# Triangular inverses in a linear-attention encoder: elimination on blocks of 16 and two joins on TensorE, in place of elimination on blocks of 32 and one join

## Chip, cores and metric

One Trainium2 chip, one of its cores. The metric is the device time of the whole program in microseconds (us); lower is better. All arithmetic is in 32-bit floats; the large products split each operand into a high and a low part and use three matmuls.

## The reference

An encoder layer runs on two sequences of 512 and 256 tokens, held together as T = 768 columns: a mixer (half RWKV-7, half gated linear attention, GLA), cross attention, and a feed-forward network. The change lies in the RWKV-7 part. Each of its 8 heads carries a 64x64 state through time, forward and backward:

```python
def step(S, inp):
    r_t, w_t, k_t, v_t, kk_t, a_t = inp
    sa = jnp.einsum('bhij,bhj->bhi', S, -kk_t)
    S = (S * w_t[:, :, None, :] + sa[..., None] * (kk_t * a_t)[:, :, None, :]
         + v_t[..., None] * k_t[:, :, None, :])
    return S, jnp.einsum('bhij,bhj->bhi', S, r_t)
```

The kernel does this in chunks of 64 tokens. Within a chunk the corrections `sa` of all tokens depend on one another through a strictly triangular 64x64 matrix L, so the kernel needs the inverse of (I - L) for every chunk, head and direction: 12 chunks x 2 heads x 2 directions for each of 4 pairs of heads.

## The kernel before

Work is written in program order and then ordered by a planner, which has a cost model of each instruction and a priority that the code sets with `tc.high_priority(offset=...)`. Each engine then runs its own list in order. All transfers go through one queue, that of SP.

The mixer handles four pairs p of heads:

- `begin(p)` prepares a pair: decays, the scaled keys `bk`, and `lower`, which makes L on TensorE (L685), copies it to the tile `lsb`, and writes its diagonal blocks to the DRAM tensor `ld`.
- `invert(p)` calls `inverses`. It loads the diagonal 32x32 blocks so that one partition holds one block (48 forward blocks on partitions 0 to 47, 48 backward ones, flipped, on 64 to 111). It builds the inverse in `sqf` by elimination on VectorE: 31 steps, each a multiply into `stmp` (L744) and an add (L746). The inverse goes to the DRAM tensor `qd`, its transpose to `td`.
- `joined(p)` calls `join`. It loads both back in the layout of the matrices (`tt` holds the 64x64 result, `tdz` a transposed block), multiplies the off-diagonal 32x32 block of L with the inverses on its two sides (L788, copied by ScalarE at L792; then L800, copied by VectorE at L803), and writes the 64x64 inverse to `ttd`.
- `products(st, g)` loads the pieces of a group of chunks from DRAM, `ttd` among them, into the tiles `pl`, and makes the matrices of the recurrence. `stage(q)` runs the recurrence over chunks in four steps (L1018 to L1064), pair q and part of pair q - 1 together.

Around them lie dense projections (`gla_dense`, `rkv_early`, L247), the four GLA heads, and 16 `memory_block`s (L1104), which the planner may put between other work. The program order of the pairs is: begin, invert and join 0; pair 1 among the GLA heads; begin and invert 2; stage 0; begin 3, join 2, invert 3; the memory blocks; stage 1; join 3; stages 2, 3 and 4. An inverse is therefore always written after the join of the pair before, with which it shares `sqf`.

The tiles `snf`, `sqf` and `sxf`, each 1,024 floats a partition, later hold weights of the output projection and its gain row `g_post`.

Of the kernel before, what the change touches and what calls it, by code (L numbers as in the profile page):

```python
# [8 lines left out]
F32 = mybir.dt.float32  # L9
F32R = mybir.dt.float32r  # L10
# [6 lines left out]
P = 128  # L17
D = 1024
# [14 lines left out]
def kernel(ctx: ExitStack, tc: tile.TileContext, I, y_prompt, y_sample):  # L33
# [354 lines left out]
    for v in ("w0_f", "w0_b", "a0_f", "a0_b", "k_k", "k_a", "lnx_w", "lnx_b"):  # L388
# [214 lines left out]

    mp_cm = tc.tile_pool(name="mp", bufs=1, reuse_waits="tile")
    mp = mp_cm.__enter__()
    tts, tdz = [], []
    for d in range(2):
        t = mp.tile([P, NCH, 64], F32, tag=f"tt{d}", name=f"tt{d}")
        pool.memset(t, 0.0)
        tts.append(t)  # L610
        tdz.append(mp.tile([P, NCH, 32], F32, name=f"tdz{d}"))
# [5 lines left out]
    sn, sq, sx = snf[0:112], sqf[0:112], sxf[0:112]  # L617
    stmp = mp.tile([112, 256], F32, name="stmp")
    pool.memset(sn, 0.0)

    def pt_(tag, bufs=1):
# [56 lines left out]
    def lower(st, d, b_, a_):  # L678

        lt = mp.tile([P, NCH, 64], F32, tag="lsb", bufs=4, name="lsb")  # L680
        for c0, n in ((0, 8), (8, 4)):
            pm = psn("low").rearrange("p (c x) -> p c x", x=64)
            for c in range(n):
                for h, hs in enumerate(HS):
                    pe.matmul(out=pm[hs, c, :], lhsT=b_[hs, c0 + c, h, :], rhs=a_[hs, c0 + c, h, :],  # L685
                              start=True, stop=True)
# [44 lines left out]
    def inverses(st):  # L731


        flat = fl
        ld, qd, td = (x[st["p"]] for x in (lds, qds, tds))
        dma(sn[0:48], ld[0].rearrange("s b c t -> (b c) s t"))
        dma(sx[64:112], ld[1].rearrange("s b c t -> (b c) s t"))
        dve.tensor_copy(out=flat(sn[64:112]), in_=flat(sx[64:112])[:, ::-1])
        dve.memset(sq, 0.0)
        dve.memset(flat(sq)[:, 0:1024:33], 1.0)  # L740
        for j in range(31):
            nr, ni = j + 1, 31 - j
            tm = stmp[:, 0:nr * ni].rearrange("p (a b) -> p a b", a=nr)
            dve.tensor_tensor(out=tm, in0=sq[:, 0:nr, j:j + 1].broadcast_to([112, nr, ni]),  # L744
                              in1=sn[:, j:j + 1, j + 1:32].broadcast_to([112, nr, ni]), op=ALU.mult)
            dve.tensor_tensor(out=sq[:, 0:nr, j + 1:32], in0=sq[:, 0:nr, j + 1:32], in1=tm, op=ALU.add)  # L746
        dma(qd[0].rearrange("s b c t -> (b c) s t"), sq[0:48])
        dve.tensor_copy(out=sn[0:48], in_=sq[0:48].rearrange("p a b -> p b a"))
        dma(td[0].rearrange("s b c t -> (b c) s t"), sn[0:48])
        dve.tensor_copy(out=flat(sx[64:112]), in_=flat(sq[64:112])[:, ::-1])  # L750
        dma(qd[1].rearrange("s b c t -> (b c) s t"), sx[64:112])
        dve.tensor_copy(out=sn[64:112], in_=sq[64:112, ::-1, ::-1].rearrange("p a b -> p b a"))
        dma(td[1].rearrange("s b c t -> (b c) s t"), sn[64:112])
    def begin(p, k_=None):
        if k_ is None:
            k_ = rk_("k")
# [13 lines left out]
            join(sts[p])  # L770

    def join(st):
        qd, td = qds[st["p"]], tds[st["p"]]
        tt, lts = tts, st["lts"]
        for d in range(2):
            for j in range(4):
                rs = slice(j * 32, j * 32 + 32)
                dma(tt[d][rs, :, (j % 2) * 32:(j % 2) * 32 + 32], qd[d][:, j])
                if j % 2 == d:
                    dma(tdz[d][rs], td[d][:, j])  # L780
        fts = []
        for d in range(2):
            o0, o1 = 32 * d, 32 - 32 * d
            pm = psn("merge1")[:, 0:NCH * 32].rearrange("p (c x) -> p c x", x=32)
            for c in range(NCH):
                for h in (0, 64):
                    ks_ = slice(h + o0, h + o0 + 32)
                    pe.matmul(out=pm[h + o1:h + o1 + 32, c, :], lhsT=lts[d][ks_, c, o1:o1 + 32], rhs=tdz[d][ks_, c, :],  # L788
                              start=True, stop=True)
            ft = sqf[:, 12 * d:12 * d + 12, :]  # L790
            for h in (0, 64):
                act.activation(out=ft[h + o1:h + o1 + 32], in_=pm[h + o1:h + o1 + 32], func=AF.Copy)  # L792
            fts.append(ft)
        for d in range(2):
            o0, o1 = 32 * d, 32 - 32 * d
            pn = psn("merge2")[:, 0:NCH * 32].rearrange("p (c x) -> p c x", x=32)
            for c in range(NCH):
                for h in (0, 64):
                    ks_ = slice(h + o1, h + o1 + 32)
                    pe.matmul(out=pn[h + o0:h + o0 + 32, c, :], lhsT=fts[d][ks_, c, :], rhs=tt[d][ks_, c, o1:o1 + 32],  # L800
                              start=True, stop=True)
            for h in (0, 64):
                dve.tensor_copy(out=tt[d][h + o0:h + o0 + 32, :, o1:o1 + 32], in_=pn[h + o0:h + o0 + 32])  # L803
# [203 lines left out]
    def step(st, x, j, pc):  # L1007
# [27 lines left out]
        if nxt:  # L1035
            for i, u in enumerate(us):
                for h, hs in enumerate(HS):
                    mark(pe.matmul(out=pr[hs, i, :], lhsT=bkt[:, u, h, :], rhs=xv[:, h, u, :], start=True, stop=True))
            t1 = mq1.tile([P, 2, 64], F32, tag="t1", bufs=3, name="t1")
            dve.tensor_tensor(out=t1, in0=pr, in1=bl(pcs[:, sl], 64), op=ALU.mult)  # L1040
            nx, nsl = nxt[0][0], nxt[1]
            for h, hs in enumerate(HS):
# [154 lines left out]
        if k != 3:  # L1197
            load_split(mixd[k], *mix[k], lo_eng=pool)
    planes = []
    for n in ("snf", "sqf"):  # L1200
        t = mp.tile([P, 2, 512], F32R, tag=n, name="w_" + n)
        planes += [t[:, 0, :], t[:, 1, :]]
# [48 lines left out]
    def out_projection(sp, wt, h, res_rows, rows, g, xd, gp):  # L1251
# [5 lines left out]
        for i in range(6):  # L1257
# [5 lines left out]
            for half in range(2):  # L1263
                pd = (psd, psy)[i % 2]("po")
                mm3(pd, [((h[k][0][:, ts_], h[k][1][:, ts_]), (wt[k][0][half], wt[k][1][half])) for k in wt])
                with tc.high_priority():
                    act.activation(out=mo[half], in_=pd, func=AF.Square, scale=1.0 / 32, accum_out=ss[:, half:half + 1])
                    dve.tensor_tensor(out=mo[half], in0=pd, in1=g[:, CS[half]], op=ALU.mult)
# [474 lines left out]
```

## Time and profile before

| what | value |
|---|---|
| median of 3 runs | 1593.78 us (1593.54 to 1599.62) |
| the profiled execution | 1596.87 us, span 1595.0 us |
| mean granted TensorE clock | 0.914 |
| VectorE's elimination (L744, L746) | 53.09 + 50.40 us, 124 instructions each |
| TensorE's join (L788, L800) | 9.45 + 8.12 us, 384 instructions each |
| ScalarE's copies in the join (L792) | 7.70 us, 16 instructions |
| VectorE's copies in the join (L803) | 8.86 us, 16 instructions |
| transfers | 279,565 packets, 89,264 of them under 512 bytes |

In the profile, PE is TensorE's matmul, PEld its weight load, DVE VectorE, ACT ScalarE, POOL GpSimd, SP the engine that issues the transfers. L744 is line 744 of the kernel. A line such as `A <- B: 8.2, 5, 4.2` under the waits says that A's engine sat idle until B, 8.2 us in total, 5 times, at most 4.2. The clock is a share of full speed.

### The profile page before, as it was taken

To read this page: it belongs to the slowest core of one execution; us is meant where nothing else is said; L and a number is where in the kernel's file an instruction comes from. 1 tells how busy PE (TensorE), PEld (TensorE's weight loads), DVE (VectorE), ACT (ScalarE), POOL (GpSimd) and SP (SyncE) were. 2 spreads that over 40 slices of the span, in tenths; PEclk is the share of its full clock that TensorE was granted. 3 is DMA by queue.
4 is the path that set the end of the run, shared out by engine and by line. 5 is a ranking of instruction groups with operands and counts; after the bars stand their busy time and mean duration, and the time that the engine had idled before them with its cause. 6 is when DMAs were issued, how large, how long until landed. Compare 5 with 4: busy or idle time off the path is not lost. (4 is left out here: it accounts for less than half of the span.)

```text
span 1595.0 us, 28271 instructions
## 1 busy us (share of the span) xinstructions
PE 1442.8 (90%) x10614; PEld 1246.0 (78%) x10614; DVE 1049.7 (66%) x1605; ACT 718.9 (45%) x1417; POOL 514.6 (32%) x576
## 2 busy tenths in 40 slices
PE   7999689889887889899888999996999999999996
PEld 6887578777775777778767888786999999787785
DVE  5545885497577795764455434448876676878886
ACT  5754344443333332333344354434555556544442
POOL 6416643494317342211531354420000001231223
PEclk9999798989875988888979999997999999999998
DMA  6686555556468447754452333235555447564434
GB/s 168 181 302 188 167 137 131 145 146 192 111 205 229 127 149 176 205 134 135 126 166 99 119 95 105 73 111 160 172 169 176 158 145 284 171 204 132 143 100 142
DMA packets 279565, 250.35 MB, mean 157 GB/s; under 512 B 89264, under 2 KB 227059, under 8 KB 279428
## 3 DMA queue, kind: packets, MB, share of 16 engines
q1 hardware_dynamic: 279428, 248.54, 52.1%
q8 instruction: 84, 1.38, 0.4%
q14 instruction: 53, 0.43, 0.1%
HBM read 164.11 MB, written 82.58 MB: 155 GB/s over the span
## 5 line engine op out<-in xcount | busy, mean ns | idle before, releaser
L148 POOL TENSOR_TENSOR wlo<-wraw,whi 128x256 fp32r<-128x256 f32 x192 | 176.8, 934 | 331.0 <-ACT whi L147 231.1
L247 PE MATMUL pd<-hT_hi,whi 128*128 128x256 f32 (+1 forms) x512 | 182.0, 356 | 12.6 <-DVE gd L325 8.2
L247 PE MATMUL pd<-hT_hi,wlo 128*128 128x512 f32 (+1 forms) x512 | 180.1, 354 | 4.0 <-POOL wlo L148 4.0
L247 PE MATMUL pd<-hT_lo,whi 128*128 128x256 f32 (+1 forms) x512 | 178.6, 350 | 0.3 <-DVE hT_lo L206 0.3
L1511 POOL TENSOR_TENSOR wl<-w,wh 128x1024 fp32r<-128x1024 f32 x8 | 21.2, 2649 | 329.8 <-ACT wh L1510 329.8
L247 PEld LDWEIGHTS pd<-hT_hi,whi 128*128 128x128 f32 x512 | 100.4, 196 | 27.6 <-issue 5.5
L247 PEld LDWEIGHTS pd<-hT_hi,wlo 128*128 128x128 f32 x512 | 99.6, 195 | 18.6 <-POOL wlo L148 5.3
L147 ACT ACTIVATE whi<-wraw 128x256 fp32r<-128x256 f32 x192 | 77.3, 414 | 78.2 <-PE pd L1104 22.9
L247 PEld LDWEIGHTS pd<-hT_lo,whi 128*128 128x128 f32 x512 | 100.4, 196 | 13.0 <-DVE hT_lo L206 0.5
L148 DVE TENSOR_TENSOR ul<-ur,uh 128x768 fp32r<-128x768 f32 x56 | 77.4, 1388 | 30.7 <-ACT uh L147 17.7
L147 ACT ACTIVATE uh<-ur 128x768 fp32r<-128x768 f32 x56 | 47.4, 847 | 107.8 <-PE gz L1520 52.0
L1510 ACT ACTIVATE wh<-w 128x1024 fp32r<-128x1024 f32 x64 | 67.1, 1053 | 35.9 <-PE fz L1520 24.2
L1520 PE MATMUL gx<-wh,uh 128*128 128x512 f32 x192 | 75.0, 397 | 4.3 <-DVE acc L1713 4.3
L1511 DVE TENSOR_TENSOR wl<-w,wh 128x1024 fp32r<-128x1024 f32 x56 | 68.2, 1219 | 15.1 <-ACT wh L1510 14.5
L1520 PE MATMUL gx<-wl,uh 128*128 128x512 f32 x192 | 75.9, 395 | 0.0
L1520 PE MATMUL gx<-wh,ul 128*128 128x512 f32 x192 | 75.4, 395 | 0.0
L1520 PE MATMUL fz<-hh,wh 128*128 128x384 f32 x192 | 66.0, 344 | 1.9 <-ACT wh L1510 1.9
L1511 POOL TENSOR_TENSOR wl<-ws,wh 128x1024 fp32r<-128x1024 f32 x16 | 40.6, 2536 | 79.6 <-ACT wh L1510 79.6
L1520 PE MATMUL fz<-hh,wl 128*128 128x384 f32 x192 | 65.2, 344 | 0.8 <-DVE wl L1511 0.8
L1520 PE MATMUL fz<-hl,wh 128*128 128x384 f32 x192 | 65.8, 343 | 0.0
L1510 ACT ACTIVATE wh<-ws 128x1024 fp32r<-128x1024 f32 x48 | 50.5, 1052 | 26.8 <-PE fx L1520 22.3
L1104 PE MATMUL pd<-mem_hi,whi 128*128 128x256 f32 x256 | 59.3, 308 | 1.4 <-ACT mo L1116 1.4
(476 smaller groups left out, 4306.9 us busy)
## 6 DMA issues: line engine op xcount, KB each, us to landing
w<-in_w_ff_dram SPq DMA_DIRECT2D x64, 512.0 KB
ur<-ud SPq DMA_DIRECT2D x56, 384.0 KB
wraw<-in_w_in_dram SPq DMA_DIRECT2D x108, 128.0 KB
ud<-u SPq DMA_DIRECT2D x32, 384.0 KB
ud<-us SPq DMA_DIRECT2D x24, 384.0 KB
wraw<-in_wkv_x_dram SPq DMA_DIRECT2D x64, 128.0 KB
lora<-lo_t SPq DMA_DIRECT2D x20, 384.0 KB
bkg<-bkd SPq DMA_DIRECT2D x24, 256.0 KB
```

Source lines behind the costliest of these rows:

```text
L147: act.activation(out=hi, in_=src, func=AF.Copy)
L148: (lo_eng or pool).tensor_tensor(out=lo, in0=src, in1=hi, op=ALU.subtract)
L247: pe.matmul(out=out, lhsT=a, rhs=b, start=(i == 0), stop=(i == n - 1))
L1104: prev = order_after(pe.matmul(out=pd[:, c0:c0 + 256], lhsT=x, rhs=y[:, c0:c0 + 256], start=(k + i + c0 == 0), stop=(k + i + c0 == KD + 25 ...
L1510: act.activation(out=hi, in_=t[name], func=AF.Copy)
L1511: lo_eng.tensor_tensor(out=lo, in0=t[name], in1=hi, op=ALU.subtract)
L1520: pe.matmul(out=out, lhsT=a, rhs=b, start=first and i == 0, stop=last and i == n - 1, skip_group_check=True)
```

## The change

Elimination works on blocks of 16, two (`e`) in one partition, so that one instruction handles both: 15 steps, 30 instructions on VectorE. The off-diagonal 16x16 blocks inside each 32x32 block are no longer part of it. `join` first makes the 32x32 inverses on TensorE. `offb` holds the off-diagonal 16x16 block, loaded from `lsb`; `inv` holds the 16x16 inverses (index 0) and their transposes (index 1) on the diagonal of 32x32 blocks with zeros elsewhere. Three products follow in each direction: `merge0` (off-diagonal block times transposed inverse, to which VectorE adds the identity), `merge0t` (the transposed 32x32 inverse, to `tdz`) and `merge0m` (the 32x32 inverse, to `tt`). ScalarE copies the last two out. The join from 32 to 64 stays, with its last copy on ScalarE in place of VectorE. The diagonal blocks are written and read in runs of 16 floats in place of 32, with 8 writes of `ld` a direction in place of 4, and with 8 loads of `inv` and 4 of `offb` in place of 4 of `tt` and 2 of `tdz`. Tiles move to make room: `snf`, `sqf`, `sxf` have half their size, `tdz` lives in `snf` and `stmp`, `t1` has two buffers in place of three, and the weight planes and the gain row lie in other tiles.

```diff
-    lds, qds, tds = ([[dp.tile([32, 4, NCH, 32], F32, name=f"{n}{p}{d}") for d in range(2)] for p in range(4)]
-                     for n in ("ld", "qd", "td"))
+    lds = [[dp.tile([2, 16, 4, NCH, 16], F32, name=f"ld{p}{d}") for d in range(2)] for p in range(4)]
+    qds = [[dp.tile([2, 16, 4, NCH, 2, 16], F32, name=f"qd{p}{d}") for d in range(2)] for p in range(4)]
...
-    snf, sqf, sxf = (mp.tile([P, 32, 32], F32, tag=n, name=n) for n in ("snf", "sqf", "sxf"))
+    snf, sqf, sxf = (mp.tile([P, 512], F32, tag=n, name=n) for n in ("snf", "sqf", "sxf"))
...
-        for j in range(4):
-            dma(lds[st["p"]][d][:, j], lt[j * 32:(j + 1) * 32, :, (j % 2) * 32:(j % 2) * 32 + 32])
+        for j in range(8):
+            c = j % 4 * 16
+            dma(lds[st["p"]][d][j % 2, :, j // 2], lt[j * 16:(j + 1) * 16, :, c:c + 16])
...
-        for j in range(31):
-            nr, ni = j + 1, 31 - j
-            tm = stmp[:, 0:nr * ni].rearrange("p (a b) -> p a b", a=nr)
-            dve.tensor_tensor(out=tm, in0=sq[:, 0:nr, j:j + 1].broadcast_to([112, nr, ni]),
-                              in1=sn[:, j:j + 1, j + 1:32].broadcast_to([112, nr, ni]), op=ALU.mult)
-            dve.tensor_tensor(out=sq[:, 0:nr, j + 1:32], in0=sq[:, 0:nr, j + 1:32], in1=tm, op=ALU.add)
+        for j in range(15):
+            nr, ni = j + 1, 15 - j
+            tm = stmp[0:112, 0:2 * nr * ni].rearrange("p (e a b) -> p e a b", e=2, a=nr)
+            dve.tensor_tensor(out=tm, in0=sq[:, :, 0:nr, j:j + 1].broadcast_to([112, 2, nr, ni]),
+                              in1=sn[:, :, j:j + 1, j + 1:16].broadcast_to([112, 2, nr, ni]), op=ALU.mult)
+            dve.tensor_tensor(out=sq[:, :, 0:nr, j + 1:16], in0=sq[:, :, 0:nr, j + 1:16], in1=tm, op=ALU.add)
...
     def join(st):
+        tdz = [t[:, 0:NCH * 32].rearrange("p (c x) -> p c x", x=32) for t in (snf, stmp)]
+        G = [slice(32 * j, 32 * j + 32) for j in range(4)]
         for d in range(2):
+            for j in range(8):
+                e, x = j % 2, j % 2 * 16
+                dma(invs[d][j * 16:j * 16 + 16].rearrange("p c q x -> p (c q) x")[:, :, x:x + 16],
+                    qd[d][e, :, j // 2].rearrange("s c q t -> s (c q) t"))
             for j in range(4):
-                rs = slice(j * 32, j * 32 + 32)
-                dma(tt[d][rs, :, (j % 2) * 32:(j % 2) * 32 + 32], qd[d][:, j])
-                if j % 2 == d:
-                    dma(tdz[d][rs], td[d][:, j])
+                r, c = 32 * j + 16 * d, j % 2 * 32 + 16 * (1 - d)
+                dma(offb[r:r + 16, d, :, 16 * (1 - d):16 * (1 - d) + 16], lts[d][r:r + 16, :, c:c + 16])
+        for d in range(2):
+            def bank(name):
+                return (psn, psm)[d](name)[:, 0:NCH * 32].rearrange("p (c x) -> p c x", x=32)
+
+            inv, fi = invs[d], (sqf, sxf)[d][:, 0:NCH * 32].rearrange("p (c x) -> p c x", x=32)
+            pm = bank("merge0")
+            for c in range(NCH):
+                for g in G:
+                    pe.matmul(out=pm[g, c, :], lhsT=offb[g, d, c, :], rhs=inv[g, c, 1, :], start=True, stop=True)
+            dve.tensor_tensor(out=fi, in0=pm, in1=bc(i32, NCH), op=ALU.add)
+            pm = bank("merge0t")
+            for c in range(NCH):
+                for g in G[d::2]:
+                    pe.matmul(out=pm[g, c, :], lhsT=inv[g, c, 0, :], rhs=fi[g, c, :], start=True, stop=True)
+            for g in G[d::2]:
+                act.activation(out=tdz[d][g], in_=pm[g], func=AF.Copy)
+            pm = bank("merge0m")
+            for c in range(NCH):
+                for g in G:
+                    pe.matmul(out=pm[g, c, :], lhsT=fi[g, c, :], rhs=inv[g, c, 0, :], start=True, stop=True)
+            for j, g in enumerate(G):
+                act.activation(out=tt[d][g, :, j % 2 * 32:j % 2 * 32 + 32], in_=pm[g], func=AF.Copy)
...
-                dve.tensor_copy(out=tt[d][h + o0:h + o0 + 32, :, o1:o1 + 32], in_=pn[h + o0:h + o0 + 32])
+                act.activation(out=tt[d][h + o0:h + o0 + 32, :, o1:o1 + 32], in_=pn[h + o0:h + o0 + 32], func=AF.Copy)
...
-            t1 = mq1.tile([P, 2, 64], F32, tag="t1", bufs=3, name="t1")
+            t1 = mq1.tile([P, 2, 64], F32, tag="t1", bufs=2, name="t1")
```

More of the change, by code (lines that the diff above doesn't have):

```diff
@@ L605 @@
     mp = mp_cm.__enter__()
-    tts, tdz = [], []
+    tts, invs, offs = [], [], []
     for d in range(2):
@@ L610 @@
         tts.append(t)
-        tdz.append(mp.tile([P, NCH, 32], F32, name=f"tdz{d}"))
+        t = mp.tile([P, NCH, 2, 32], F32, tag=f"inv{d}", name=f"inv{d}")
+        pool.memset(t, 0.0)
+        invs.append(t)
+    offb = mp.tile([P, 2, NCH, 32], F32, tag="offb", name="offb")
+    pool.memset(offb, 0.0)
+    i32 = mp.tile([P, 32], F32, name="i32")
+    for j in range(4):
+        rs = slice(32 * j, 32 * j + 32)
+        pool.tensor_copy(out=i32[rs], in_=ident[rs, rs])
     px = mp.tile([P, NCH, 66], F32, tag="px", name="px")
@@ L615 @@
     px_prev = (px[:, :, 0:64], px[:, :, 2:66])
-    snf, sqf, sxf = (mp.tile([P, 32, 32], F32, tag=n, name=n) for n in ("snf", "sqf", "sxf"))
-    sn, sq, sx = snf[0:112], sqf[0:112], sxf[0:112]
-    stmp = mp.tile([112, 256], F32, name="stmp")
+    snf, sqf, sxf = (mp.tile([P, 512], F32, tag=n, name=n) for n in ("snf", "sqf", "sxf"))
+    sn, sq, sx = (t[0:112].rearrange("p (e a b) -> p e a b", e=2, a=16) for t in (snf, sqf, sxf))
+    stmp = mp.tile([P, NCH * 32], F32, tag="stmp", name="stmp")
     pool.memset(sn, 0.0)
@@ L731, in inverses @@
     def inverses(st):
[L734 to L737, printed above, removed]
-        dve.tensor_copy(out=flat(sn[64:112]), in_=flat(sx[64:112])[:, ::-1])
-        dve.memset(sq, 0.0)
-        dve.memset(flat(sq)[:, 0:1024:33], 1.0)
-        for j in range(31):
-            nr, ni = j + 1, 31 - j
-            tm = stmp[:, 0:nr * ni].rearrange("p (a b) -> p a b", a=nr)
-            dve.tensor_tensor(out=tm, in0=sq[:, 0:nr, j:j + 1].broadcast_to([112, nr, ni]),
-                              in1=sn[:, j:j + 1, j + 1:32].broadcast_to([112, nr, ni]), op=ALU.mult)
-            dve.tensor_tensor(out=sq[:, 0:nr, j + 1:32], in0=sq[:, 0:nr, j + 1:32], in1=tm, op=ALU.add)
@@ L747, in inverses, with flat, rows16, put @@
-        dma(qd[0].rearrange("s b c t -> (b c) s t"), sq[0:48])
-        dve.tensor_copy(out=sn[0:48], in_=sq[0:48].rearrange("p a b -> p b a"))
-        dma(td[0].rearrange("s b c t -> (b c) s t"), sn[0:48])
+        ld, qd = lds[st["p"]], qds[st["p"]]
+        def flat(t):
+            return t.rearrange("p e a b -> p (e a b)")
+        def rows16(t):
+            return t.rearrange("p e s t -> p (e s) t")
+        def put(d, q, t):
+            dma(qd[d].rearrange("e s j c q t -> (j c) (e s) q t")[:, :, q, :], rows16(t))
@@ new lines, in inverses @@
+        for d, t in enumerate((sn[0:48], sx[64:112])):
+            dma(rows16(t), ld[d].rearrange("e s j c t -> (j c) (e s) t"))
+        dve.tensor_copy(out=flat(sn[64:112]), in_=flat(sx[64:112])[:, ::-1])
+        dve.memset(flat(sq), 0.0)
+        for e in range(2):
+            dve.memset(flat(sq)[:, 256 * e:256 * e + 256:17], 1.0)
+        for j in range(15):
[4 more added lines that the diff above has]
+            dve.tensor_tensor(out=sq[:, :, 0:nr, j + 1:16], in0=sq[:, :, 0:nr, j + 1:16], in1=tm, op=ALU.add)
@@ L750, in inverses @@
+        put(0, 0, sq[0:48])
+        dve.tensor_copy(out=sn[0:48], in_=sq[0:48].rearrange("p e a b -> p e b a"))
+        put(0, 1, sn[0:48])
         dve.tensor_copy(out=flat(sx[64:112]), in_=flat(sq[64:112])[:, ::-1])
-        dma(qd[1].rearrange("s b c t -> (b c) s t"), sx[64:112])
-        dve.tensor_copy(out=sn[64:112], in_=sq[64:112, ::-1, ::-1].rearrange("p a b -> p b a"))
-        dma(td[1].rearrange("s b c t -> (b c) s t"), sn[64:112])
+        put(1, 0, sx[64:112])
+        dve.tensor_copy(out=sn[64:112], in_=sq[64:112, ::-1, ::-1, ::-1].rearrange("p e a b -> p e b a"))
@@ L754, in begin @@
+        put(1, 1, sn[64:112])
     def begin(p, k_=None):
@@ L789, in join @@
                               start=True, stop=True)
-            ft = sqf[:, 12 * d:12 * d + 12, :]
+            ft = (sqf, sxf)[d][:, 0:NCH * 32].rearrange("p (c x) -> p c x", x=32)
             for h in (0, 64):
@@ L1199 @@
     planes = []
-    for n in ("snf", "sqf"):
-        t = mp.tile([P, 2, 512], F32R, tag=n, name="w_" + n)
-        planes += [t[:, 0, :], t[:, 1, :]]
+    for n, w in (("snf", 512), ("sqf", 512), ("inv0", T), ("inv1", T)):
+        planes.append(mp.tile([P, w], F32R, tag=n, name="w_" + n)[:, 0:512])
     for g in (0, 4, 1, 5):
@@ L1267, in out_projection @@
                     act.activation(out=mo[half], in_=pd, func=AF.Square, scale=1.0 / 32, accum_out=ss[:, half:half + 1])
-                    dve.tensor_tensor(out=mo[half], in0=pd, in1=g[:, CS[half]], op=ALU.mult)
+                    dve.tensor_tensor(out=mo[half], in0=pd, in1=g[half], op=ALU.mult)
             with tc.high_priority():
@@ L1284, in out_projection @@
         return hh, hl
-    g_post = mp.tile([P, D], F32, tag="sxf", name="g_post")
-    dma(g_post, I["g_mix_post"].broadcast_to([P, D]))
+    g_post = [mp.tile([P, w], F32, tag=n, name="g_post")[:, 0:512] for n, w in (("sxf", 512), ("offb", T))]
+    for g_, cs in zip(g_post, CS):
+        dma(g_, I["g_mix_post"][:, cs].broadcast_to([P, 512]))
     with tc.tile_pool(name="op1", bufs=1, reuse_waits="tile") as op1:
```

3 lines of the change are left out of this document (1 added, 2 removed).

## The prediction

> **What bounds the kernel now.** I read the page's busy shares first, then the busy time by stretch, then TensorE's waits over the mixer, and last the instructions that the change touches.
>
> ```profile
> span 1595.0 us, 28271 instructions
> PE 1442.8 (90%) x10614; PEld 1246.0 (78%) x10614; DVE 1049.7 (66%) x1605; ACT 718.9 (45%) x1417; POOL 514.6 (32%) x576
> ```
>
> TensorE is busy nine tenths of the span and VectorE two thirds. The change takes work from the second and gives work to the first, so the average speaks against it. What counts is the mixer, where the inverses lie. The columns below are stretch, length, then busy time of PE, PEld, DVE, ACT and POOL, the granted clock, and the DMA share and rate.
>
> ```profile
> 110.00:200.00 90.00, 72.25 (x480) 60.57 (x479) 60.73 (x47) 37.95 (x68) 56.02 (x54) 0.85 0.66 191
> 200.00:300.00 100.00, 89.13 (x672) 75.10 (x672) 59.20 (x102) 43.88 (x80) 37.49 (x50) 0.90 0.54 137
> 300.00:430.00 130.00, 114.97 (x736) 97.58 (x736) 103.07 (x132) 58.74 (x105) 75.41 (x63) 0.86 0.54 144
> 430.00:560.00 130.00, 108.53 (x1419) 90.69 (x1417) 94.82 (x175) 46.39 (x124) 57.24 (x50) 0.76 0.66 186
> 560.00:650.00 90.00, 78.08 (x1108) 66.64 (x1108) 63.46 (x147) 30.12 (x80) 27.74 (x27) 0.88 0.68 181
> 650.00:760.00 110.00, 102.84 (x1382) 88.37 (x1384) 70.27 (x192) 40.29 (x112) 18.44 (x25) 0.84 0.53 142
> 760.00:880.00 120.00, 104.27 (x781) 82.75 (x782) 63.60 (x132) 48.53 (x131) 40.87 (x68) 0.90 0.42 131
> sum 770.00, PE 670.07 PEld 561.70 DVE 515.14 ACT 305.90 POOL 313.22; mean PE 95.72 PEld 80.24 DVE 73.59 ACT 43.70 POOL 44.75
> ```
>
> From 110 to 880 us TensorE is busy 670 of 770 us (87%), VectorE 515 (67%), ScalarE 306 (40%). So 100 us of TensorE idle time is all that a lighter VectorE can give back here, and anything new on TensorE competes for a nearly full engine. Who releases TensorE from its waits in the same stretch:
>
> ```profile
> PE low L685 <- DVE bk L672: 16.6, 5, 6.8
> PE rec L1049 <- DVE t L1040: 8.2, 5, 4.2
> PE pd L247 <- DVE gd L325: 8.2, 3, 4.9
> ...
> PE rec L1031 <- DMA pl<-ttd: 5.4, 2, 4.6
> ...
> PE merge L788 <- DMA tdz<-td: 3.6, 4, 1.3
> ```
>
> The columns are total, count and longest. VectorE is the main releaser. The largest row is bk at L672, part of preparing a pair, which comes before its inverse. The inverse of an earlier pair can delay it only where the two overlap. The row on ttd is the one that says "the inverse came too late": the recurrence waits for the joined inverse, 5.4 us in all.
>
> **The change part by part.** *VectorE, the elimination.* The four inverses' multiplies and adds go through the tile stmp; here are its instructions in the stretch of each pair (after the bounds and the length, VectorE's busy time and count; 62 is 31 multiplies and 31 adds):
>
> ```profile
> 208.00:254.30 46.30, 26.97 (x62) 0.96 0.52 137
> 377.00:419.00 42.00, 25.63 (x62) 0.87 0.42 112
> 527.00:610.00 83.00, 26.58 (x62) 0.81 0.44 128
> 643.00:695.00 52.00, 24.32 (x62) 0.90 0.59 174
> ```
>
> Together 103.5 us for 248 instructions, 25.9 us a pair. Single instructions from the timeline (start, length):
>
> ```profile
> 208.97 0.19 DVE L744 TENSOR_TENSOR stmp<-sqf,snf 112x31 f32<-112x31 f32 x1
> 214.67 0.30 DVE L744 TENSOR_TENSOR stmp<-sqf,snf 112x135 f32<-112x135 f32 x1
> 251.30 1.14 DVE L748 COPY snf<-sqf 48x1024 f32<-48x1024 f32 x1
> 252.47 0.69 DVE L750 COPY sxf<-sqf 48x1024 f32<-48x1024 f32 x1
> ```
>
> From 31 and 135 elements: 1.06 ns an element and 0.157 us fixed. Old, a pair: 62 instructions on 10,912 elements (twice the sum of (j+1)(31-j)), 9.7 + 11.6 = 21.3 us; the trace has 25.9, a factor of 1.22 for slow instances. New: 30 instructions on 2,720 elements, 4.7 + 2.9 = 7.6 us, times 1.22 is 9.2. Saved: 16.7 us a pair. Six-tenths of the inverse's work goes (16.7/25.9 = 64%). The four copies (two like L748, two like L750, 3.6 us) halve with the tile, 1.8 saved. The memset halves too, which I leave out.
>
> *VectorE against ScalarE in the join.* Further rows:
>
> ```profile
> L803 DVE COPY tt<-merge x16: 545/553/565, 283.9 to 730.7; 32x384 f32<-32x384 f32 x16
> L792 ACT ACTIVATE sqf<-merge x16: 463/482/485, 265.6 to 721.5; 32x384 f32<-32x384 f32 x16
> L41 SPq DMA_DIRECT2D tt<-qd x32: 409/467/1657, 256.8 to 707.8; - x32
> ```
>
> L803, four a pair, leaves VectorE: 2.2 us. Two additions of the identity come, 128x384 from PSUM; as long as L803, 1.1 us. VectorE in all: 16.7 + 1.8 + 2.2 - 1.1 = 19.6 us a pair, 78 us of its 515. ScalarE gains 16 copies a pair (4 for tdz, 8 for tt, 4 for the old L803), 16 x 0.48 = 7.7 us a pair, 31 in all; at 40% busy it has room, but in each join they lie between one product and the next.
>
> *TensorE.* Per pair and direction merge0 has 48 products, merge0t 24, merge0m 48. In the trace a product is two instructions: L788 has 192 products and 384 matmuls. So 240 a direction, 480 a pair, 1,920 in all. Their price, from join 0:
>
> ```profile
> L788 PE MATMUL merge<-tdz,lsb x384: 191/191/258, 261.0 to 720.7; 32*32 32x32 f32 x192
> ...
> 261.85 0.94 PE L788 MATMUL merge<-tdz,lsb 32*32 32x32 f32 x46 [0.56 <-DMA tdz<-td]
> ...
> 273.19 1.49 PE L788 MATMUL merge<-tdz,lsb 32*32 32x32 f32 x48
> 274.61 0.80 PE L247 MATMUL pd<-hT_hi,wlo 128*128 128x512 f32 x1
> ```
>
> Less the last one's length, (0.94 - 0.19)/45 = 16.7 ns each at speed, and (1.49 - 0.26)/47 = 26 ns in a slow-clock passage; mean 21.4. Upper bound: 1,920 x 21.4 = 41 us. Those rows use two array tiles by turns; merge0 and merge0m use four, merge0t two. If four tiles run at twice the rate, 384 x 21.4 + 1,536 x 10.7 = 24.7 us, the lower bound. I take the middle, 33, as no row shows four. Some falls into TensorE's idle time; at its 13% share 4 us, leaving 29 on the path.
>
> The Trainium skill ("TensorE: Matmul & The Clock Gate", Part 1, on the 56 ns gap) says that matmul starts never come closer than about 25 ns, however small. The row above does not agree: 16.7 ns between starts on two tiles. By the rule the sum's TensorE term would be 48 us in place of 33, the forecast 13 us later; by its Part 3, that tiles in different row groups overlap, the lower bound would hold.
>
> *Hand-overs.* Each direction gains three steps in which TensorE's result goes to another engine and back. The old join left waits only at its first product (L788 on tdz, 3.6 us in 4 waits, 0.9 each). 24 new ones at 0 to 0.9: 0 to 22 us. I take 2, as the old copies at L792 left TensorE no listed wait, other work lying between. If that filler is gone the price is 22. The join's first merge now waits in TensorE's queue, so everything queued behind, products and recurrence, waits with it.
>
> *Clock.* The matmul after the slow merge takes 0.80 us. More passages of tiny products with waits between them might hold the clock low longer: 0 to 2 us for each of 4 joins, as a 512-column product at 0.80 instead of the half of it loses 0.4 us and some five follow each other; near the lower end, as only one of the quoted passages was slow: 2.
>
> *SP and DMA.* Per pair 8 more writes of ld, and 16 + 8 loads in the join against 12: 20 more issues at 0.47 us, 9.4 us of SP's queue, 38 in all, ahead of weight and place loads. The runs shrink from 128 to 64 bytes; counted from the patterns there are 9,984 packets in place of 7,744 a pair and direction. Cost on the path 0 to 19 us (half of the issues); I take 0, since weights are loaded ahead; the cover is their buffers, and if it is gone it is the third rival.
>
> *Relief.* TensorE's waits inside the inverse's stretches (first, second and third pair):
>
> ```profile
> PE gvt L463 <- DVE gd L325: 2.6, 2, 1.9
> PE pd L247 <- DVE gd L325: 1.5, 1, 1.5
> PE pd L247 <- DVE gd L465: 1.5, 2, 1.0
> ...
> PE go L913 <- DVE arena L904: 4.7, 1, 4.7
> PE pd L247 <- DVE gd L465: 1.9, 1, 1.9
> ...
> PE rec L1049 <- DVE t L1040: 4.2, 1, 4.2
> PE sca L989 <- DVE pl L996: 3.0, 1, 3.0
> PE low L685 <- DVE bk L672: 3.0, 2, 1.9
> PE rec L1018 <- DVE pl L995: 1.9, 1, 1.9
> ```
>
> They sum to 24.3 us. The 4.7 goes back to a GLA scan, so 19.6 remain; at 64%, 13 us back (bounds 0 and 24.3). The wait on ttd, 5.4: 4 back, the join itself being longer. What is late next there is the join's own chain. Fewer gaps lift the clock, worst in 430-560 at 0.76. At 0.85 its 108.5 us would be 97, a gain of 11, bound 0 below; I take 5. Third buffer of t1, moved gain rows, weight planes: VectorE both writes and reads t1, and the planes become free with the last join; nothing, at most 1 us.
>
> **The sum:** 29 (TensorE) + 2 (hand-overs) + 2 (clock lost) - 13 (waits in the inverses) - 4 (ttd) - 5 (clock won) = +11 us. The profiled execution took 1596.9 us (span 1595.0); the median of the runs is 1593.8, 3.1 lower. I add 11 to the median: 1605 us.
>
> **The rivals.** *Faster:* VectorE's queue is what spoils the mixer. Place: stretches 208-254 and 527-610. All 24.3 + 5.4 us of waits go, the clock gains 11, and TensorE pays the low price in part from its idle time (24.7 x 0.87 = 21.5): -19, 1575 us. It decides once relief and clock exceed TensorE's price. For it speak the 33 us of waits in the three quoted rows on VectorE over the mixer; against it, that TensorE has only 13% left. *No change:* low price, forecast relief: 21.5 + 2 + 2 - 13 - 4 - 5 = +3, 1597 us. *SP's queue:* late loads add 19 to +11: 1624 us. For it, the 38 us of issues; against, that loads run ahead. *The elimination does not shrink as stated:* four-dimensional patterns cost more an instruction; at the old mean of 0.417 us (103.5/248) 30 take 12.5, 52% of the inverse goes in place of 64%, relief falls by 3: 1608 us.
>
> **How the numbers follow.** Forecast 0.34, SP 0.08, no shrink 0.04, no change 0.27, faster 0.27. Differences within 0.5%, 8 us, are about what a measurement of this kernel tells from none. Slower 0.46, same 0.27, faster 0.27. The range, 1578 to 1626, cuts the faster rival's end and the hand-overs' worst case; slower alone is 1602 to 1626.
>
> **What would show it.** 120 eliminations of 0.19 to 0.3 us, about 37 us in all; TensorE's new merge rows at 25 to 41 us; ScalarE 31 us more; the waits on t, pl and gd in the inverse's stretches shorter; ttd's wait gone. Wrong, if merges cost under 20 us or fill idle time, if the clock from 430 to 560 rises past 0.85, or if the planner's new order moves waits elsewhere.

## The result, and the profile after

The changed kernel took 1680.85 us (median of 4 runs, 1676.61 to 1683.18) beside 1595.54 for the kernel before: a ratio of 1.055 [1.0521, 1.0578], 85 us slower. The forecast was 1605 us, with a range of 1578 to 1626. The direction was right; the size missed by 76 us and the range by 55. The profiled execution has a span of 1680.1 us and a mean granted clock of 0.899 (before 0.914).

The busy times moved nearly as forecast, as the page shows:

```profile
span 1680.1 us, 32202 instructions
PE 1491.3 (89%) x12534; PEld 1290.6 (77%) x12534; DVE 976.2 (58%) x1473; ACT 749.4 (45%) x1481; POOL 500.0 (30%) x583
```

VectorE lost 73.5 us (forecast 78), ScalarE gained 30.5 (31). TensorE's new merges, each line alone from 110 to 880 us (busy time and count of PE, then of PEld): merge0, merge0t, merge0m:

```profile
110.00:880.00 770.00, 12.34 (x768) 10.18 (x768) 0.82 0.52 139
110.00:880.00 770.00, 8.36 (x384) 7.38 (x384) 0.82 0.52 139
110.00:880.00 770.00, 10.23 (x768) 8.64 (x768) 0.82 0.52 139
```

They sum to 30.9 us (forecast 33, bounds 25 to 41). The waits that the prediction watched shrank in part: L1098 on t is 3.4 us (as L1049 before: 8.2), low on bk 11.1 (16.6), and the recurrence's wait on ttd is gone. From 110 to 880 us TensorE waited 52 us for VectorE in place of 61, and yet its idle time there rose from 100 to 110 us, since other waits came. TensorE's waits after, over the whole span, total, count and longest:

```profile
PE po L247 <- POOL mix_px L148: 22.5, 1, 22.5
PE sca L1038 <- DMA pl<-ard: 16.6, 1, 16.6
PE low L695 <- DVE bk L682: 11.1, 3, 7.9
PE merge0m L827 <- issue: 10.9, 6, 2.5
PE merge L816 <- DMA inv<-qd: 8.1, 6, 3.5
PE merge0t L821 <- issue: 5.6, 3, 2.1
...
PE rec L1098 <- DVE t L1089: 3.4, 2, 2.1
```

The two largest stand before stage 0's scores (sca) and before the output projection (po). Where the lateness begins is read from three groups, the first product of the GLA heads (gs), their scans, and the scores, with first and last start after the durations. Before, then after:

```profile
L862 PE MATMUL gs<-arena x192: 218/267/366, 143.1 to 372.5; 64*64 64x64 f32 x192
L903 DVE TENSOR_TENSOR_SCAN arena<-arena x4: 3350/3391/3870, 183.7 to 402.5; 64x1536 f32<-64x1536 f32 x4
L989 PE MATMUL sca<-pl,bkg x192: 269/269/473, 440.8 to 773.0; 64*64 64x128 f32 x192
```

```profile
L911 PE MATMUL gs<-arena x192: 218/267/366, 245.8 to 466.1; 64*64 64x64 f32 x192
L952 DVE TENSOR_TENSOR_SCAN arena<-arena x4: 3349/3350/3350, 265.7 to 481.5; 64x1536 f32<-64x1536 f32 x4
L1038 PE MATMUL sca<-pl,bkg x192: 269/269/473, 529.7 to 830.8; 64*64 64x128 f32 x192
```

Head 0's product moved from 143 to 246 us, and stage 0's scores from 441 to 530: 89 us, about the whole loss, before the recurrence has begun. The 89 are not carried whole to the end: the last scores are 58 us late, and the wait of 22.5 us before the output projection comes on top. Stage 0's tiles lie in the memory that the heads' `arena` gives back, so it cannot begin before the last head ends. The timeline after, around head 0 (start, length):

```profile
236.67 0.90 PE L827 MATMUL merge0m<-inv,sqf 32*32 32x32 f32 x83 [0.28 <-ACT snf L823]
240.10 0.28 PE L827 MATMUL merge0m<-inv,sqf 32*32 32x32 f32 x11 [2.52 <-issue]
...
244.10 0.48 PE L827 MATMUL merge0m<-inv,sxf 32*32 32x32 f32 x19 [2.36 <-issue]
...
244.78 1.96 ACT L829 ACTIVATE tt<-merge0m 32x384 f32<-32x384 f32 x4 [1.36 <-PE merge0m L827]
245.76 1.36 PEld L911 LDWEIGHTS gs<-arena 64*64 64x64 f32 x24
```

Head 0's products follow join 0's last product of the second direction. The code says why. `psn` and `psm` hand out PSUM banks, the places that products are written to: `psn` has one (bank n in the texts below), `psm` a ring of two by turns (banks m). `bank` gives the second direction a bank of `psm`, and `gs` takes two of the same ring (`pfb = [psm("gs") ... for _ in range(2)]`). Join 0 is written before head 0, join 1 before head 2, so the heads' banks come after the joins'. Before, the join used only `psn`. The joins end late, as an inverse and a trip through memory stand ahead of them, and now heads 0 and 2 wait for them.

The clock, forecast to gain in 430 to 560, fell there from 0.76 to 0.72, but that stretch now lies mostly ahead of the scores and holds other work; over the scores' own stretches (441 to 775 before, 530 to 832 after) it is 0.82 in both. From 880 to 960 TensorE had been busy throughout and now stands still for 22.5 us, the wait named above. After, then before for 880 to 960, then the end of that wait in the timeline after:

```profile
430.00:560.00 130.00, 103.84 (x784) 85.86 (x782) 85.43 (x121) 53.87 (x109) 64.47 (x59) 0.72 0.57 159
...
880.00:960.00 80.00, 57.51 (x254) 46.27 (x254) 42.74 (x71) 31.35 (x80) 28.96 (x50) 0.85 0.46 143
```

```profile
880.00:960.00 80.00, 79.07 (x465) 68.94 (x464) 30.05 (x65) 37.42 (x98) 37.72 (x56) 1.00 0.37 110
```

```profile
903.04 1.19 PE L247 MATMUL po<-w_snf,mix_bk 128*128 128x512 f32 x2 [22.49 <-POOL mix_px L148]
```

### The profile page after: what moved, and what is told of

It is laid out like the page before. It is cut to its first block, busy times and chain, and to the rows that moved or that the text cites. A ratio compares the mean times of both kernels' runs of the same rounds, so it can differ in the third digit from the quotient of the medians.

```text
span 1680.1 us, 32202 instructions
## 1 busy us (share of the span) xinstructions
PE 1491.3 (89%) x12534; PEld 1290.6 (77%) x12534; DVE 976.2 (58%) x1473; ACT 749.4 (45%) x1481; POOL 500.0 (30%) x583
## 4 chain that ended last, share of the span: by engine, by line
PE 61%; DVE 13%; issue 9%; DMA 8%; SPq 3%; POOL 3%; ACT 3%; DVEq 0%; POOLq 0%; ACTq 0%
PE pd L247 12%; PE fx L1569 7%; PE gx L1569 6%; PE fz L1569 5%; PE gz L1569 5%; PE pd L1153 4%; SPq L41 3%; PE po L247 3%; PE go L962 1%; DMA wraw<-in_w_in_dram 1%; PE hsum L641 1%; PE rec L1067 1%; PE xo L247 1%; PE sca L1038 1%; DVE ws L1509 1%
## 5 line engine op out<-in xcount | busy, mean ns | idle before, releaser
L148 POOL TENSOR_TENSOR wlo<-wraw,whi 128x256 fp32r<-128x256 f32 x192 | 164.7, 869 | 440.4 <-ACT whi L147 355.8
L247 PE MATMUL pd<-hT_hi,whi 128*128 128x256 f32 (+1 forms) x512 | 189.8, 371 | 12.0 <-DVE gd L325 4.3
L247 PE MATMUL pd<-hT_hi,wlo 128*128 128x512 f32 (+1 forms) x512 | 186.0, 366 | 3.3 <-POOL wlo L148 3.3
L247 PE MATMUL pd<-hT_lo,whi 128*128 128x256 f32 (+1 forms) x512 | 185.2, 363 | 0.3 <-DVE hT_lo L206 0.3
L247 PEld LDWEIGHTS pd<-hT_hi,whi 128*128 128x128 f32 x512 | 105.3, 206 | 27.7 <-issue 4.3
L247 PEld LDWEIGHTS pd<-hT_hi,wlo 128*128 128x128 f32 x512 | 104.7, 205 | 19.7 <-POOL wlo L148 5.8
L247 PEld LDWEIGHTS pd<-hT_lo,whi 128*128 128x128 f32 x512 | 105.3, 206 | 14.4 <-issue 0.9
L1560 DVE TENSOR_TENSOR wl<-w,wh 128x1024 fp32r<-128x1024 f32 x56 | 68.2, 1219 | 16.6 <-ACT wh L1559 16.1
L1559 ACT ACTIVATE wh<-ws 128x1024 fp32r<-128x1024 f32 x48 | 50.4, 1052 | 27.3 <-PE fx L1569 22.5
L1153 PE MATMUL pd<-mem_hi,wlo 128*128 128x256 f32 x256 | 62.5, 317 | 0.0
```

What stands on the lines that cost most here:

```text
L148: (lo_eng or pool).tensor_tensor(out=lo, in0=src, in1=hi, op=ALU.subtract)
L247: pe.matmul(out=out, lhsT=a, rhs=b, start=(i == 0), stop=(i == n - 1))
L1153: prev = order_after(pe.matmul(out=pd[:, c0:c0 + 256], lhsT=x, rhs=y[:, c0:c0 + 256], start=(k + i + c0 == 0), stop=(k + i + c0 == KD + 25 ...
L1559: act.activation(out=hi, in_=t[name], func=AF.Copy)
L1560: lo_eng.tensor_tensor(out=lo, in0=t[name], in1=hi, op=ALU.subtract)
```

## The experiments

Theory A: the loss is the shared bank. Theory B: it is the work of the merges and their hand-overs. As the planner makes a new order for every kernel, later ones are controls of the order. A "tie" is a dependency that fixes the order of two groups on TensorE; the tied preparation, inverse or join is also written later in the program, so that the planner's order changes elsewhere too. "Half the elimination" leaves out every second step and "without those products" leaves out the off-diagonal 16x16 blocks; both give incomplete inverses.

| kernel | median us | beside before | ratio |
|---|---|---|---|
| e1: the change, all merges in psn | 1626.39 | 1589.73 | 1.0234 [1.0196, 1.0272] |
| e2: before, old merges' second direction in psm | 1623.04 | 1589.73 | 1.0214 [1.0181, 1.0247] |
| e5: before plus the products of the first join | 1704.12 | 1589.73 | 1.0723 [1.0686, 1.0759] |
| e6: e1 without those products | 1640.05 | 1589.73 | 1.0316 [1.0278, 1.0355] |
| e7: before, half the elimination | 1623.23 | 1591.41 | 1.0202 [1.015, 1.0255] |
| e8: before, another priority | 1602.13 | 1591.41 | 1.0064 [1.0031, 1.0096] |
| e9: e1, another priority | 1656.99 | 1591.41 | 1.0396 [1.0358, 1.0435] |
| e3: before, L803's copies on ScalarE | 1593.91 | 1591.41 | 1.0011 [0.9988, 1.0033] |
| e10: e7, one tie | 1616.36 | 1593.23 | 1.0156 [1.0102, 1.0211] |
| e11: e6, one tie | 1609.18 | 1593.23 | 1.0113 [1.0087, 1.014] |
| e12: the change, one tie | 1698.57 | 1593.23 | 1.0676 [1.0652, 1.0701] |
| e13: before, two ties | 1606.30 | 1591.21 | 1.011 [1.0069, 1.0151] |
| e14: e7, two ties | 1624.23 | 1591.21 | 1.0203 [1.0165, 1.024] |
| e15: e6, two ties | 1626.76 | 1591.21 | 1.0246 [1.0202, 1.0289] |
| e16: e1, two ties | 1646.40 | 1591.21 | 1.0349 [1.032, 1.0378] |
| e17: before, four ties | 1617.95 | 1593.13 | 1.015 [1.0109, 1.0191] |
| e18: e7, four ties | 1616.52 | 1593.13 | 1.0143 [1.0116, 1.017] |
| e19: e1, four ties | 1633.22 | 1593.13 | 1.0233 [1.0182, 1.0284] |

**The bank.** e1 takes it out of the change, e2 puts it into the kernel before.

```diff
 # e1, in the change
-                return (psn, psm)[d](name)[:, 0:NCH * 32].rearrange("p (c x) -> p c x", x=32)
+                return psn(name)[:, 0:NCH * 32].rearrange("p (c x) -> p c x", x=32)
 # e2, in the kernel before, for merge1 and merge2
-            pm = psn("merge1")[:, 0:NCH * 32].rearrange("p (c x) -> p c x", x=32)
+            pm = (psn, psm)[d]("merge1")[:, 0:NCH * 32].rearrange("p (c x) -> p c x", x=32)
```

> The changed kernel with one edit: the second direction's three new products use the single PSUM bank 'n', like the first direction's, in place of the two banks 'm' that the GLA heads use. Theory A (banks): in the changed kernel the first GLA head's product gs waits for a bank 'm' that join 0, written before it, must use first; the heads' chain and the tiles of stage 0, which lie in the memory of the last head, come some 82 us late. With the edit gs of head 0 starts before 150 us again and the time falls by 60 to 85 us, to 1596-1620 us. Theory B (work: the 1,920 matmuls, their hand-overs and slower clock, as the prediction priced them, only dearer): the time stays within 15 us of 1681, or grows, since one bank serves both directions.

> The kernel before with only the banks changed: the second direction's two products of the join (merge1, merge2) use the banks 'm' in place of 'n'. No instruction is added or removed. Theory A: gs of head 0 moves behind join 0 and starts at 250 to 290 us in place of 143; the time grows by 50 to 90 us, to 1645-1685 us. Theory B: a bank more makes the hand-overs shorter; 1585 to 1600 us.

The same groups in e1:

```profile
L911 PE MATMUL gs<-arena x192: 218/218/337, 147.2 to 398.1; 64*64 64x64 f32 x192
L952 DVE TENSOR_TENSOR_SCAN arena<-arena x4: 3349/3824/4446, 189.0 to 417.2; 64x1536 f32<-64x1536 f32 x4
L1038 PE MATMUL sca<-pl,bkg x192: 269/269/473, 454.7 to 813.9; 64*64 64x128 f32 x192
```

And in e2:

```profile
L862 PE MATMUL gs<-arena x192: 218/218/367, 257.4 to 460.3; 64*64 64x64 f32 x192
L903 DVE TENSOR_TENSOR_SCAN arena<-arena x4: 3349/3521/4831, 281.8 to 492.9; 64x1536 f32<-64x1536 f32 x4
L989 PE MATMUL sca<-pl,bkg x192: 269/269/472, 535.2 to 812.8; 64*64 64x128 f32 x192
```

One word moves head 0's product from 246 back to 147 us in the change (time -54 us) and from 143 on to 257 in the kernel before (+33 us). The bank is shown as a cause in both directions, though both times moved less than theory A gave (60 to 85 and 50 to 90 us). It is not a constant price: e2's scores are 94 us late and its end only 33. TensorE was no fuller ahead of the scores in e2 (busy 345 of the 425 us from 110 to 535) than in the changed kernel (340 of 420), so why e2 makes up more stays open. One difference is known: the changed kernel's wait of 22.5 us before the output projection is neither in e1 nor in e2, while e6 and e7 below, which do not use the second bank, have one of 24.0 and 23.3. It comes with an order of the planner, and some of e1's 54 us may be this wait and not the bank. Of the change, 36.7 us are left in e1.

**The products alone.** e5 adds the first join's products, additions and 12 copies a join to the kernel before, on bank n and with results that nobody uses. e6 leaves them out of e1.

```diff
 # e5, at the head of join, for each direction
+            pm = bank("x0")
+            for c in range(NCH):
+                for j, g in enumerate(G):
+                    pe.matmul(out=pm[g, c, :], lhsT=lts[d][g, c, cw(j)], rhs=tt[d][g, c, cw(j)], start=True, stop=True)
...
 # e6, in join
-                act.activation(out=tdz[d][g], in_=pm[g], func=AF.Copy)
+                act.activation(out=tdz[d][g], in_=inv[g, :, 1, :], func=AF.Copy)
...
```

> The kernel before with TensorE's and ScalarE's share of the change added and nothing taken away: in each join 240 extra products, two additions on VectorE and 12 copies on ScalarE, all in bank 'n', whose results nothing uses; the elimination stays on blocks of 32. Theory A with the prediction's prices: TensorE's 29 us, 2 for hand-overs, 2 for clock, no relief: +33 us, 1622 to 1635 us. Theory B: +75 us or more, since the work itself is what made the change slow.

> The changed kernel with bank 'n' (as in the first run) and without the three new products and the addition: ScalarE copies the inverses of 16 straight to tt and tdz. It leaves out the off-diagonal 16x16 blocks, so that what remains is the lighter elimination with its transfers and copies. Theory A with the prediction's prices: relief of 13 + 4 + 5 us and no cost, 1570 to 1580 us, some 30 to 35 us under the first run. Rival: the elimination was never what TensorE waited for, and the time is that of before, 1590 to 1600 us.

e6 misses both theories; e5's time is the one that theory B gave (75 us or more), against A. But B's reason does not fit e1, which holds the same products and is 37 us over before, nor e6: adding the products cost 114 us, and leaving them out of e1 made it 14 us slower. No sum of busy times does this: e6 has one wait of 24.0 us of the output projection on GpSimd's splits and one of 15.2 of the scores on a transfer, which e1 lacks. These kernels differ in the planner's order as well as in work. In e5 the loss lies inside the recurrence: its first scores start 22 us late and its last 115 late, and the added products wait 33 us in all (22 of it at the first of the three), where the like products of e1 wait 2.7. Where the rest of the 114 comes from stays open.

**Order alone, and relief alone.** e8 and e9 change a priority and no instruction; e7 lightens the elimination and changes nothing else; e3 is one part of the change alone.

```diff
 # e7, before
-        for j in range(31):
+        for j in range(0, 31, 2):
 # e8, before, in invert
-        with tc.high_priority(offset=2000):
+        with tc.high_priority(offset=3000):
 # e9, e1, in joined
-        with tc.high_priority(offset=6000):
+        with tc.high_priority(offset=2500):
 # e3, before, L803
-                dve.tensor_copy(out=tt[d][h + o0:h + o0 + 32, :, o1:o1 + 32], in_=pn[h + o0:h + o0 + 32])
+                act.activation(out=tt[d][h + o0:h + o0 + 32, :, o1:o1 + 32], in_=pn[h + o0:h + o0 + 32], func=AF.Copy)
```

> The kernel before with every second step of the elimination left out (32 instructions of VectorE a pair in place of 62; the inverses are then incomplete); products, banks and transfers stay. It has only the relief that the change brings. Theory A (a lighter elimination saves what the prediction took off for it): 1575 to 1585 us. Rival B (the lighter elimination makes the planner put the instructions into another order, and that order has stalls of its own: scores of stage 0 behind transfers on SP's queue, the output projection behind splits on GpSimd, as in e6, whose products stand at the same places of TensorE's order): 1610 to 1640 us, with both stalls in the waits at 10 us or more.

> The kernel before with the priority offset of the four inverses at 3000 in place of 2000: the same instructions, in the same order up to stage 0, in another one from stage 1 on. A control for what the planner's order alone is worth. If order alone is worth little: 1585 to 1597 us. If it is worth tens of us: outside 1580 to 1605 us.

> e1 (all merges in bank n) with the priority offset of the joins at 2500 in place of 6000: the same instructions, in the same order up to the last GLA head, in another one from stage 0 on. If order alone is worth little: 1616 to 1636 us, as e1. If the remaining 36 us of e1 are an unlucky order and not the merges: more than 15 us off e1, to either side.

> The kernel before with the four copies of the second half of each join (line 803) on ScalarE in place of VectorE: one part of the change alone. ScalarE is busy 45% of the span, so the copies are covered: 1585 to 1597 us by the theory that the banks and the merges are the loss. Rival, that the copies hold up the joins or shift the planner's order: above 1600 us.

The copies are free (e3, no difference that can be measured). Order alone is worth some 10 us in e8, between its two cases, and 26 (by the ratios) to 31 us (by the medians) in e9. And the relief, 13 us of gain in the prediction, ran 32 us slower by itself. It is only a part of the change's relief: e7 takes 33 us off VectorE's busy time, the change 73.5. e7's waits and TensorE's timeline ahead of stage 0:

```profile
PE low L685 <- DVE bk L672: 25.7, 7, 7.4
PE po L247 <- POOL mix_px L148: 23.3, 1, 23.3
```

```profile
469.53 0.41 PE L463 MATMUL gvt<-ident,gd 128*128 128x128 f32 x2 [1.92 <-DVE gd L325]
477.36 1.65 PE L685 MATMUL low<-bk 64*64 64x64 f32 x26 [7.42 <-DVE bk L672]
478.70 0.47 PE L989 MATMUL sca<-pl,bkg 64*64 64x128 f32 x1
```

With VectorE free earlier, the planner moved pair 2's preparation ahead of stage 0, and TensorE, which runs its list in order, stood 7.4 us before pair 2's low with stage 0's scores behind it (479 in place of 441 us; before, pair 2's low came behind the first scores). Of the two waits that I expected, only the projection's came above 10 us.

**With the order held.** The tie of e10 to e12 puts low of pair 2 behind the scores of pair 0's group 5. e13 to e16 also put join 1 behind GLA head 3, e17 to e19 also join 0 behind head 1 and low of pair 1 behind head 2's gs.

```diff
 # first tie
-                    pe.matmul(out=pm[hs, c, :], lhsT=b_[hs, c0 + c, h, :], rhs=a_[hs, c0 + c, h, :],
+                    x = pe.matmul(out=pm[hs, c, :], lhsT=b_[hs, c0 + c, h, :], rhs=a_[hs, c0 + c, h, :],
...
+                    if st["p"] == 2 and first:
+                        order_after(x, first[-1])
 # second tie, on the join's first products
+                    if st["p"] == 1:
+                        order_after(x, gone[-1])
```

> e7 (the kernel before with half the elimination steps left out) with pair 2 begun behind the first scores of stage 0 in the program, and its products low tied behind the scores of group 5 of pair 0 on TensorE. In e7 the planner had put low of pair 2 ahead of stage 0, where TensorE waited 7.4 and 5.4 us for VectorE. If that place is what made a lighter elimination cost 32 us: scores of stage 0 start at 440 to 460 us (e7: 479) and the time is 1575 to 1600 us. If it is the tail (output projection behind splits of GpSimd, 23 us) that costs: that wait stays above 15 us and the time stays at 1610 to 1630 us.

> e6 (the change in bank n, without the products of the first join, the off-diagonal 16-blocks left out) with the same tie as e10. Theory: without bank and order trouble the change minus its merges runs at the time before or under it, and e1's 36 us are the merges: 1575 to 1600 us. Rival: the finer transfers, the shared tiles or the copies cost in themselves: 1610 us or more, with transfers (DMA) as the releasers of the new waits.

> The changed kernel with the same tie as e10 and nothing else: both banks stay. In the changed kernel low of pair 2 stands at 465 to 471 us, ahead of stage 0's scores at 530 us. If its place is a second cause beside the banks: scores of stage 0 at 500 to 515 us, 1645 to 1665 us. If the GLA heads, late by the banks, alone set stage 0: 1672 to 1690 us, as the changed kernel.

The tie took 31 us off e6, where the wait of 24.0 us on the splits went; e11 lies between the two ranges. Off e7 it took 7 us (intervals that overlap): e10's time is that of the second case, but the projection's wait on GpSimd is down to 2.1 us, so neither case holds. In the change (e12) the scores began at 513 us in place of 530, as the first case has it, and the time still rose by 18 us: an earlier stage 0 is no earlier end by itself, and moving pair 2 behind it does not win back any of the change's loss.

> The kernel before, its work unchanged, with two ties of TensorE's order: products low of pair 2 behind the scores of group 5 of pair 0 (begin and invert of pair 2 written behind those scores), and the products of join 1 behind the last products go of GLA head 3 (join 1 written behind that head). The baseline of a set of four kernels with the same ties. Its order up to stage 0 is that of before: 1585 to 1605 us by both theories; beyond 1610 the ties themselves cost.

> e13 with half of the elimination steps left out: the relief alone, with the two ties. Theory A (e7 and e10 were slow because the lighter elimination let the planner put join 1 ahead of GLA head 3 and low of pair 2 ahead of stage 0, and both are now tied): at or under e13, by 0 to 15 us, scores of stage 0 at 435 to 450 us. Rival B (something else of the lighter elimination costs): 15 us or more over e13, as e10 was over before.

> The change in bank n without the products of the first join (off-diagonal 16-blocks left out), with the two ties. Theory A: the finer transfers, shared tiles and copies are nearly free: within 10 us of e14. Rival B: they cost 15 us or more over e14.

> The whole change, all merges in bank n, with the two ties. Theory A (the merges lie on the path with nearly all of TensorE's 31 us): 20 to 32 us over e15, so 1600 to 1625 us. Rival B (they fill idle time of TensorE): under 12 us over e15.

The two ties cost 15 us by themselves (e13). Against this baseline, the set prices the parts: half the elimination +18 us (e14 less e13), the rest of the relief with transfers, shared tiles and copies +3, which the intervals do not tell from nothing (e15 less e14), merges +20 by the medians and 16 by the ratios (e16 less e15, at 25.4 us more busy time of TensorE). So e14 met B and e15 met A; e16 met the difference that theory A gave and not its absolute range. Relief still lost, and so did the whole of it with transfers, tiles and copies: e15 is 20 us over e13. In e14 the heads' products are again pushed back (last start, e13, then e14):

```profile
L866 PE MATMUL gs<-arena x192: 218/218/367, 143.4 to 369.1; 64*64 64x64 f32 x192
```

```profile
L866 PE MATMUL gs<-arena x192: 218/218/366, 144.1 to 388.3; 64*64 64x64 f32 x192
```

In e14 pair 1's low begins at 300 us (e13: 322) and join 0 ends at 264 (287), so both have moved ahead of heads on TensorE. The last set ties those as well.

> e13 (the kernel before with two ties) with two more: the first product of join 0 behind the last product go of GLA head 1, and low of pair 1 behind the last product gs of GLA head 2, with begin and invert of pair 1 and join 0 written behind those heads. Baseline for e18 and e19. 1590 to 1615 us by all theories.

> e17 with half the elimination steps left out: the relief alone, with TensorE's order of GLA heads, joins 0 and 1 and low of pairs 1 and 2 held as in e17. e14 cost 18 us over e13. Theory A (the lighter elimination lost because freed VectorE time lets the next pair's preparation and the joins go ahead of the GLA heads on TensorE): within 6 us of e17 or under it. Rival B (it loses for another reason, or by order later than stage 0): 10 us or more over e17.

> The whole change, all merges in bank n, with the four ties. Theory A: e17 plus the merges' 20 us (e16 less e15), so 1610 to 1635 us. Rival B (the ties don't help the change): 1640 us or more, as e16.

e17 is 25 us over the kernel before, 3 over its range: the four ties cost. Half the elimination now costs nothing and brings nothing (-1 us, theory A); the change is 15 us over e17 (theory A again). From 110 to 880 us, e17 and then e18 (busy time of PE, PEld, DVE, ACT, POOL):

```profile
110.00:880.00 770.00, 650.58 (x6474) 547.51 (x6475) 507.24 (x899) 295.82 (x676) 306.63 (x324) 0.85 0.56 155
```

```profile
110.00:880.00 770.00, 652.60 (x6485) 546.26 (x6483) 470.83 (x787) 299.45 (x683) 303.37 (x328) 0.85 0.56 156
```

VectorE has 36 us less to do and TensorE does 2 us more in the same stretch. Its waits there change places:

```profile
PE low L685 <- DVE bk L672: 22.8, 6, 7.3
PE pd L247 <- DVE gd L325: 12.7, 3, 6.0
PE rec L1027 <- DVE ya L1070: 10.9, 3, 7.6
PE rec L1027 <- DVE ya L1073: 8.6, 7, 3.4
...
PE rec L1058 <- DVE t L1049: 4.8, 6, 1.4
```

```profile
PE low L685 <- DVE bk L672: 28.5, 7, 7.3
PE rec L1058 <- DVE t L1049: 12.5, 11, 2.7
PE pd L247 <- DVE gd L325: 8.6, 3, 4.9
...
PE rec L1027 <- DVE ya L1073: 5.9, 4, 2.7
PE rec L1027 <- DVE ya L1070: 4.4, 3, 3.1
```

The first fence is e17, the second e18. TensorE waits 9 us less for ya and 4 less for gd, and 13 more for bk and t. All rows together, its waits on VectorE fall from 83 to 72 us, and those on ScalarE and transfers rise from 31 to 42: it looks as if, with one releaser earlier, another one ends the wait. The ties did not hold every place (e18's scores still start at 458 us, e17's at 441). So I call it shown that half the elimination's work taken away gains nothing in four settings: +32 us over before (e7), +23 over before with a tie whose own cost was not measured (e10), +18 and -1 over baselines with the same ties (e14, e18). That the planner's order makes the difference between them is likely, but not isolated.

No version beat the kernel before. The best forms of the change are e1 and e19, both 2.3% slower.

## Why the prediction was wrong

The step that failed first is one that isn't there: "The change part by part" goes through engines, waits and transfers, and not through the PSUM banks that the new products are written to. The line `(psn, psm)[d](name)` was in the diff. The closing condition "if the planner's new order moves waits elsewhere" names the case and gives it no price. It was 54 us in the change (e1) and 33 put into the kernel before (e2), the largest part of the loss; none of the rivals has it. The sum for "Hand-overs", 2 with a bound of 22, asks what is queued behind the join on TensorE, but not who shares its banks. Without the second bank the 2 was about right: the joins' products wait 4.7 us in e1 and 3.6 before. In the changed kernel they wait 26.9, of which 18.5 with "issue" as releaser. That the direction came out right is in part luck: of what made the loss, only the merges stand in the forecast's sum.

The second is "Relief" with its companions, -13, -4 and -5. The waits on VectorE did shrink in the changed kernel (61 to 52 us), and yet the relief gained no time in any kernel. A wait on VectorE inside an inverse's stretch was taken as a wait caused by the inverse. e18 shows that with half of the elimination gone most of the waits come back on other rows, and the clock from 430 to 560 is 0.78 in e1, whose stages lie near those of before, in place of 0.76, not 0.85. Setting these 22 us to zero turns the forecast's +11 into +33; e1 measured +36.7, but that closeness proves little, as the same work in another order (e9) is 66 us over before.

The third is only a size: TensorE's 33 gross was right (30.9 busy), the share lost in idle time was put at 4 and was more: in place of 29, 16 to 20 us reach the end (e16 less e15), at or under the edge of "if merges cost under 20 us".

Right were the elimination (33.5 us where "about 37" were named), ScalarE's 31, and, as far as e15 less e14 tells (3 us, with the copies and the rest of the relief in it), transfers, t1 and the moved planes at nothing; packets rose by 19,360, forecast 17,920. The rule of the Trainium skill weighed in the prediction ("TensorE: Matmul & The Clock Gate", Part 1, no starts closer than 25 ns) does not agree here either: 83 matmuls of merge0m in 0.90 us on four tiles, less the last one's 0.19, are 8.7 ns from start to start. What its Part 3 says, that tiles in different row groups overlap, agrees: that is half of the 16.7 ns on two tiles.

The account of the 85 us is rough, as the runs differ in order too, and order alone was worth 10 us in e8 and up to 31 in e9: bank 33 to 54, merges 15 to 20, relief 0 to +18, other parts about 3.

## What to carry to other kernels

Before pricing the instructions of a change, list which buffers its outputs take and who else rotates through the same ring: with two banks and program order fixing the turns, a new user that ends late holds up whatever is written after it, however short its own work. Where a planner orders the work, making an engine lighter changes the order of all others; price "relief" by what would start earlier on the path, not by the waits that it removes, and keep a control that changes a priority alone (here 10 and 26 to 31 us) beside each experiment. When a large part of a loss stands before a stage begins, compare first and last starts of a few groups ahead of any busy time.

## What the runs showed of the hardware

In the changed kernel, runs of tiny products stop for 0.3 to 2.5 us with "issue" as the only releaser: 10.9 us in 6 stops at merge0m, 5.6 in 3 at merge0t. Between the stops that end at 240.10 and 244.10 us, the timeline has 128 matmuls and 128 weight loads, 256 instructions, done within about 1.6 us. The Trainium skill ("Runtime: NRT & Kernel Launch", Instruction fetch mechanics) says that instructions are fetched in blocks of 256 and that this is hidden, as issue is slower than the fetch. The count agrees with the block; that it is hidden does not agree with these stops.

The trace has a row for this fetch, before and then after:

```profile
q8 instruction: 84, 1.38, 0.4%
```

```profile
q8 instruction: 99, 1.62, 0.4%
```

The 15 more packets, of 16,384 bytes each, are 256 instructions a packet for the 3,840 matmuls and weight loads that the change adds. Each of the nine stops ends 2.3 to 3.0 us after such a packet began to move (at 237.62 and 241.77 us for the two above). A packet alone does not stop TensorE: the next one, at 245.30 us, has no stop behind it, and e1, with 99 packets too, has no such row at its merges, which lie more among other work. So I take it that TensorE stands where it uses up 256 instructions before the next packet is there; no run took the stops apart, so this cause is inferred.
